# Output projections with tokens on the partitions: w_out and the FFN's down projection of a two-layer hybrid trunk

## The chip, the cores and the metric

The kernel runs on one core of one Trainium2 chip, as one program. The metric is the device time of a run, in microseconds (us). The kernel before takes 2708.34 us, the median of 3 runs (2707.84 to 2708.45).

## The reference

Two layers over 512 latent tokens with 256 context tokens ahead of them, width 1024. Each layer is a token-mixing sub-layer (an S5 state-space branch, windowed attention, a gated linear recurrence called HGRN2; merged by gates and put through `w_out`) and a convolutional FFN (2816 wide). Layer 0 gives 768 tokens (context and latent), layer 1 only the 512 latent ones. What matters here is what follows the two output projections: the norm of the result, its gain and gate, and the residual.

```python
def rmsnorm(x, g):
    return x * lax.rsqrt(jnp.mean(x * x, axis=-1, keepdims=True) + EPS) * g

def conv_ffn(h, w_up, conv_w, conv_b, w_down):
    u = depthwise_conv(h @ w_up, conv_w, conv_b)
    a, g = jnp.split(u, 2, axis=-1)
    return (jax.nn.silu(a) * g) @ w_down

for l in range(DEPTH):                      # latent tokens; the context rows go the same way in layer 0
    mod_l = jax.nn.silu(c) @ w_mod[l] + b_mod[l]
    sh1_l, sc1_l, g1_l, sh2_l, sc2_l, g2_l = jnp.split(mod_l, 6, axis=-1)
    hl = modulate(rmsnorm(xl, norm_g[l, 0]), sh1_l, sc1_l)
    ol, oc = mixing_sublayer(hl, hc, ...)   # ends with  @ w_out[l]
    xl = xl + g1_l * rmsnorm(ol, norm_g[l, 1])
    hl = modulate(rmsnorm(xl, norm_g[l, 2]), sh2_l, sc2_l)
    xl = xl + g2_l * rmsnorm(conv_ffn(hl, ...), norm_g[l, 3])
return xl
```

## The kernel before

Every fp32 product is made of three matmuls (hi by hi, lo by hi, hi by lo); `wload` brings a 128 by 1024 block of weights by DMA into a ring of three buffers `wr`, ScalarE writes its high part `wh`, VectorE the low part `wl` (three buffers each). All DMAs are issued by one queue on SyncE, in program order: one that waits holds up those behind it. Instructions are emitted by Python generators that `weave` interleaves at given paces, and a scheduler then sets each engine's order by priorities (`high_priority`, `lowly`); an engine works strictly in that order. All instructions are recorded by one helper line (L120; L118 in the changed kernel), so groups are told apart by tile names: `mm` and `mc` are PSUM for 512 and 256 columns, `pa` a two-bank PSUM tile, `pb` a PSUM bank with a single buffer, `slot` one of 52 SBUF buffers, `cst` the identity, `mscr` the scratch output of the modulation products, `rs_y`, `rs_v`, `rs_u`, `rs_h`, `xsv` small tiles of the reciprocal root, `cad`, `bbd`, `kd`, `tod`, `mt`, `mid` data of the S5 set-up.

The activations lie transposed, features on the partitions. In `w_out` and in the down projection the weights are stationary and the tokens stream: 512 latent columns into `mm` and, in layer 0, 256 context columns into `mc`. For `w_out` the first five blocks of output features go this way; the last three, and the last of the six groups of the down projection (`FG`, groups of 4, 4, 4, 4, 3, 3 blocks of 128 FFN features), go through `tail`: the weights are kept by `hold` in slots, and the tokens go in spans of 256 (two latent, then context), so that the residual of the first span can begin while the others are computed. The earlier groups of the down projection are summed in SBUF (`part`), one VectorE addition per block.

`out_evac` squares each block on ScalarE, scales it by the gain (modulation gate times norm weight, `amod`, one number per partition) on ScalarE and adds the squares up on VectorE (`oacc`). Features 0 to 511 are transposed back by TensorE as soon as they are there. `residual` then, for each pair of token tiles (a group), has TensorE sum the squares over the partitions by matmuls with `ones` into `pb`, transposes features 512 to 1023, and VectorE computes the reciprocal root (`mean_rstd`) and adds onto x. In three of the four cases the next norm follows (`x_scale`, `norm_part`): squares on ScalarE, a root, a scaling on VectorE, transposes, and then the next sub-layer's first products.

Two fillers run beside this. `mods_rows` computes modulation rows on VectorE; in layer 0's HGRN2 they are woven in at 1.6 per step, their weights coming through the `wr` ring. In layer 0's FFN `s5_setup(1)` gets 26 units of VectorE cost per up projection (`fs`), and then `s5_prep(1)` follows, 28 steps each of which loads blocks of `cad` and transposes them in a `pa` tile. The whole `prep` is drained by the end of the FFN.

## Time and profile before

| | us |
|---|---|
| median of 3 runs | 2708.34 |
| profiled execution: its time | 2715.15 |
| profiled execution: its span, first to last instruction | 2713.3 |
| TensorE busy | 2532.4 (93% of the span) |
| VectorE busy | 1898.0 (70%) |
| ScalarE busy | 1022.4 (38%) |
| mean granted TensorE clock | 0.976 of 2.4 GHz |

TensorE's busy time is that of overlapping, pipelined matmuls, so what a matmul costs is read from the start of one run of them to the start of the next, and what is missing from 100% is idle time, shown in brackets with its releaser. The stages follow each other in time: HGRN2 of layer 0 at about 340 to 700 us, its `w_out` at 880 to 960, its FFN at 1015 to 1600, the residual and norm that lead to layer 1 at 1600 to 1650, layer 1's FFN at 2350 to 2706.

### The profile page before, as it was taken

The page shows a single profiled execution, that of the slowest core. Times are in us where ns is not written, and L with a number is a line of the kernel's source. Part 1 is how long each engine was busy: PE and PEld are TensorE (multiplying, and loading weights), DVE is VectorE, ACT ScalarE, POOL GpSimd, SP SyncE. Part 2 cuts the span into 40 slices and gives each one's busy share as a digit, 9 for nine tenths or more (in the row PEclk, how much of TensorE's full clock was granted, in tenths as well). Part 3 has the DMA queues.
Part 4 walks back from the last instruction along what each step waited for, and adds up shares of the span by engine and source line. Part 5 has one row for each costly group of instructions (what it writes and reads, how often), then busy time and mean ns, then how long its engine had stood idle before and what let it go on. Part 6 is the DMA issues. An engine that isn't in the chain of part 4 may idle for free. (4 is left out here: it accounts for less than half of the span.)

```text
span 2713.3 us, 47072 instructions
## 1 busy us (share of the span) xinstructions
PE 2532.4 (93%) x18436; PEld 2128.1 (78%) x18436; DVE 1898.0 (70%) x4304; ACT 1022.4 (38%) x1813; POOL 121.1 (4%) x182
## 2 busy tenths in 40 slices
...
GB/s 245 128 129 112 140 143 161 148 177 134 180 197 213 111 133 142 163 117 125 119 142 144 118 136 215 147 82 92 105 117 131 168 214 163 146 95 97 98 95 99
DMA packets 239758, 381.36 MB, mean 141 GB/s; under 512 B 53648, under 2 KB 135984, under 8 KB 239536
## 3 DMA queue, kind: packets, MB, share of 16 engines
...
## 5 line engine op out<-in xcount | busy, mean ns | idle before, releaser
L120 PE MATMUL mm<-slot,wh 128*128 128x512 f32 (+1 forms) x3798 | 1200.7, 394 | 39.6 <-DVE slot L120 20.5
L120 PEld LDWEIGHTS mm<-slot,wh 128*128 128x128 f32 x3798 | 699.7, 190 | 177.2 <-DVE slot L120 24.9
L120 PE MATMUL mm<-slot,wl 128*128 128x512 f32 (+1 forms) x1899 | 742.7, 391 | 0.9 <-DVE wl L120 0.9
L120 DVE TENSOR_TENSOR slot<-slot,slot 128x384 f32<-128x384 f32 (+17 forms) x1340 | 665.8, 535 | 103.8 <-ACT slot L120 64.6
L120 PE MATMUL mc<-slot,wh 128*128 128x256 f32 (+1 forms) x3082 | 667.5, 310 | 12.8 <-ACT slot L120 10.2
L120 PEld LDWEIGHTS mc<-slot,wh 128*128 128x128 f32 x3082 | 519.0, 193 | 60.4 <-ACT slot L120 13.3
L120 DVE TENSOR_TENSOR wl<-wr,wh 128x1024 fp32r<-128x1024 f32 (+1 forms) x274 | 333.9, 1219 | 242.0 <-ACT wh L120 239.7
L120 ACT ACTIVATE wh<-wr 128x1024 fp32r<-128x1024 f32 (+1 forms) x274 | 288.5, 1053 | 525.9 <-PE mc L120 362.8
L120 PE MATMUL mc<-slot,wl 128*128 128x256 f32 (+1 forms) x1541 | 474.7, 308 | 0.0
L120 PEld LDWEIGHTS mm<-slot,wl 128*128 128x128 f32 x1899 | 360.6, 190 | 73.4 <-issue 2.6
L120 ACT ACTIVATE slot<-slot 128x768 fp32r<-128x768 f32 (+5 forms) x253 | 168.5, 669 | 383.3 <-DVE slot L120 329.7
L120 PEld LDWEIGHTS mc<-slot,wl 128*128 128x128 f32 x1541 | 297.4, 193 | 12.5
L120 PEld LDWEIGHTS pa<-slot,slot 128*32 128x32 f32 (+2 forms) x5696 | 212.5, 131 | 119.7 <-issue 60.5
L120 PE MATMUL pa<-slot,slot 128*32 128x32 f32 (+8 forms) x5696 | 254.6, 225 | 51.8 <-DVE slot L120 17.9
L120 ACT ACTIVATE slot<-mm 128x512 f32<-128x512 f32 (+1 forms) x180 | 103.6, 576 | 328.3 <-PE mm L120 288.2
L120 ACT ACTIVATE slot<-pa 128x512 f32<-128x512 f32 (+7 forms) x250 | 115.7, 493 | 238.3 <-PE pa L120 213.3
L120 PE MATMUL pa<-cst,slot 128*128 128x128 f32 x900 | 138.2, 282 | 30.6 <-DVE slot L120 20.4
L120 PEld LDWEIGHTS pa<-cst,slot 128*128 128x128 f32 x900 | 106.0, 144 | 58.3 <-issue 26.7
L120 PE MATMUL mm<-slot,slot 128*128 128x256 f32 (+1 forms) x784 | 110.7, 320 | 18.8 <-DVE xsv L120 16.2
L120 DVE SCALAR_TENSOR_TENSOR slot<-slot,slot 128x256 f32<-128x256 f32 (+7 forms) x129 | 92.4, 722 | 39.8 <-ACT slot L120 39.1
L120 DVE CUSTOM_DVE_ANT_0 mscr<-slot,slot 128x768 bf16<-128x768 f32 (+1 forms) x160 | 109.9, 687 | 14.3 <-DMA slot<-in_wmodt 12.0
L120 PEld LDWEIGHTS mm<-slot,slot 128*128 128x128 f32 (+1 forms) x784 | 92.9, 185 | 23.8 <-issue 18.2
...
## 6 DMA issues: line engine op xcount, KB each, us to landing
...
```

Source lines behind the costliest of these rows:

```text
L120: return _f(*(x.ap if isinstance(x, Slot) else x for x in a), **{k: x.ap if isinstance(x, Slot) else x for k, x in kw.items()})
```

## The change

Both output projections turn round: a block of 128 tokens of the activations is stationary, the weights stream, 512 output features at a time, and the result has tokens on the partitions. `out_proj` does `w_out` for each half of the features `f` and each pair of blocks `c`; `down` does one group for each half `f`, all token tiles, into `pa` tiles. A square with its row sum is then one ScalarE instruction (`accum_out`), and no transpose back and no sum over partitions is needed. The gain now varies along the columns: `out_state` transposes `amod` by two matmuls in `pb`, writes the rows to DRAM and loads them back onto all 128 partitions, and VectorE multiplies by them. `hold`, `tail`, `sums` and their buffers go. `FG` becomes 4, 4, 4, 4, 4, 2. Layer 0's modulation rows load into slots instead of the ring, are woven at 3 per step instead of 1.6 and drained by the end of the second head. `s5_prep(1)` uses `pb` and 4 blocks a step (36 steps), and `fs` is 22. Weights are laid out for this on the host.

```diff
-FG = [4, 4, 4, 4, 3, 3]
-DPER = {1: 8, 2: 4, 3: 2, 4: 2}
+FG = [4, 4, 4, 4, 4, 2]
...
-TL = (3, 3)
...
     def residual(self, l, which, oe, t0, nxt=None):
-            pso = self.pb()
-            self.sums(pso, oacc[0], g, True, False)
-            self.sums(pso, oacc[1], g, False, True)
-            y = self.mean_rstd(pso[:, g[0]:g[-1] + 1], len(g), "o")
-            pt = self.pa()
-            for j, t in enumerate(g):
-                for k in range(4):
-                    nc.tensor.transpose(pt[:, 512 * j + P * k:512 * j + P * k + P], o[4 + k][:, P * t:P * t + P], self.ident)
+            v = self.t(self.sm, [P, 8], "rsv")
+            nc.vector.tensor_add(v[:, :len(g)], ss[:, 0, g[0]:g[-1] + 1], ss[:, 1, g[0]:g[-1] + 1])
+            y = self.mean_rstd(v[:, :len(g)], len(g), "o")
+            o0 = {}
             for j, t in enumerate(g):
                 for f in range(2):
-                    src = pt[:, 512 * j:512 * j + 512] if f else o0[t]
-                    nc.vector.scalar_tensor_tensor(x[t][f], src, y[:, j:j + 1], x[t][f], ALU.mult, ALU.add)
+                    nc.vector.scalar_tensor_tensor(x[t][f], o[t, f], y[:, j:j + 1], x[t][f], ALU.mult, ALU.add)
                     dst = self.out[t - 2] if nxt is None else xd[t]
                     nc.sync.dma_start(dst[:, 512 * f:512 * f + 512], x[t][f])
+                o0[t] = o.pop((t, 0))
+                del o[t, 1]
...
+    def out_state(self, l, which, t0):
...
+        nv = 2 if t0 == 0 else 1
+
+        pt = self.pb()
+        a = self.s3(n=P)
+        gd = self.dr.tile([2, D], F32, name=self.nm("gain"))
+        for t in range(nv):
+            r = slice(32 * t, 32 * t + KT)
+            nc.tensor.matmul(pt[r, 0:P], self.amod[l][:, j, :, t], self.ident, start=True, stop=True)
+            nc.scalar.activation(a[r], pt[r, 0:P], AF.Copy)
+            nc.sync.dma_start(gd[t].rearrange("(k p) -> k p", p=P), a[r])
+        gain = {}
+        for t in range(nv):
+            for f in range(2):
+                gain[t, f] = self.s3(n=512)
+                nc.sync.dma_start(gain[t, f], gd[t, 512 * f:512 * f + 512].partition_broadcast(P))
+        return {"o": {}, "ss": self.t(self.sm, [P, 2, 8], "oss"), "gain": gain,
+                "groups": [range(s.start // P, s.stop // P) for s in self.spans(t0)]}
+
+    def out_evac(self, p, t, f, oe, part=None):
+
+        nc = self.nc
+        sq = self.s3(n=512)
+        o = oe["o"][t, f] = self.s3(n=512)
...
-            oe[0].pop(k, None)
+            for a, b, d in part:
+                nc.vector.tensor_add(o[:, a:b], d, p[:, a:b])
+            p = o
+        nc.scalar.activation(sq, p, AF.Square, accum_out=oe["ss"][:, f, t:t + 1])
+        nc.vector.tensor_mul(o, p, oe["gain"][0 if t >= 2 else 1, f])
+
+    def rows_product(self, out, x, w, j, t, first, last):
+
+        xh, xl = x
+        tk = slice(P * t, P * t + P)
+        wc = slice(512 * j, 512 * j + 512)
+        for i, (xt, wt) in enumerate(((xh, w[0]), (xl, w[0]), (xh, w[1]))):
+            self.nc.tensor.matmul(out, xt[:, tk], wt[:, wc], start=first and i == 0, stop=last and i == 2)
+
+    def out_proj(self, l, ms, oe):
+
+
+        groups = oe["groups"]
+        for f in range(2):
+            ps = {}
+            for g in groups:
+                if g[0] >= 2:
+                    pt = self.pa()
+                    for i, t in enumerate(g):
+                        ps[t] = pt[:, 512 * i:512 * i + 512]
+                else:
+                    for t in g:
+                        ps[t] = self.m1()
+            ws = []
+            for c in range(4):
+                ws.append(self.wload(self.I["wout"][l, f, c]))
+                if f == 0 or c == 0:
+                    for g in groups:
+                        for t in g:
+                            for j in range(2):
+                                self.rows_product(ps[t], ms[2 * c + j], ws[c], j, t, c + j == 0, 2 * c + j == KT - 1)
+                            if c == 3:
+                                self.out_evac(ps[t], t, f, oe)
+                    ws[c] = None
+            if f == 1:
+                for g in groups:
+                    for t in g:
+                        for c in range(1, 4):
+                            for j in range(2):
+                                self.rows_product(ps[t], ms[2 * c + j], ws[c], j, t, False, 2 * c + j == KT - 1)
+                        self.out_evac(ps[t], t, f, oe)
...
-        oe = {}, {}, []
-        for k in range(KT - TL[l]):
-            w = self.wload(I["wout"][l, k])
...
+        oe = self.out_state(l, 0, t0)
+        self.out_proj(l, ms, oe)
...
+        def down(gi, acts, oe=None):
             nonlocal chunk
             n = len(acts)
...
+            if gi == 0:
+                part.extend(self.s3() for _ in range(-(-4 * (NTILE - t0 // P) // 3)))
+            for f in range(2):
+                ws = [self.wload(I["wdn"][l, chunk + c]) for c in range(n // 2)]
+                chunk += n // 2
+                for g in groups:
+                    pt = self.pa()
+                    for x, t in enumerate(g):
+                        p = pt[:, 512 * x:512 * x + 512]
+                        for k in range(n):
+                            self.rows_product(p, acts[k], ws[k // 2], k % 2, t, k == 0, k == n - 1)
+                        if oe is not None:
+                            self.out_evac(p, t, f, oe, pieces(t, f))
+                            continue
+                        for a, b, d in pieces(t, f):
+                            if gi == 0:
+                                nc.scalar.activation(d, p[:, a:b], AF.Copy)
+                            else:
+                                nc.vector.tensor_add(d, d, p[:, a:b])
...
-            self.prep = self.lowly(self.s5_prep(1, self.pa, 8, self.sp), w["pb"])
+            self.prep = self.lowly(self.s5_prep(1, self.pb, 4, self.sp), w["pb"])
...
-        down(len(FG) - 1, prev)
+        oe = self.out_state(l, 1, t0)
+        down(len(FG) - 1, prev, oe)
+        part.clear()
...
-            mods = self.mods_rows(0, [i for i in range(4, 12) if i not in MLATE], 2, self.s3, True)
+            mods = self.mods_rows(0, [i for i in range(4, 12) if i not in MLATE], 2, self.s3)
...
-            self.weave(main, *g, (fill, w["hg"]), (prep, w["hp"]), (mods, 1.6))
+            self.weave(main, *g, (fill, w["hg"]), (prep, w["hp"]), (mods, 3))
+            if hh == 1:
+                self.drain(mods)
```

How it moves instructions, at the three places that matter. First TensorE at the end of layer 0's FFN. Before, the transposes of the first group's normed rows (`pa<-cst`) stand among the last products of the tail (`mm<-slot,slot`):

```order
L120 MATMUL mm_16697<-slot_2341_15953,slot_2414_16419 128x256
L120 MATMUL mm_16697<-slot_2358_16093,slot_2413_16418 128x256
L120 MATMUL mm_16697<-slot_2359_16094,slot_2413_16418 128x256
L120 MATMUL pa_16797<-cst,slot_2403_16377 128x128 [waits DVE_49,PE_49]
L120 MATMUL mm_16697<-slot_2358_16093,slot_2414_16419 128x256
L120 MATMUL pa_16797<-cst,slot_2404_16379 128x128 [waits DVE_49]
L120 MATMUL pa_16797<-cst,slot_2403_16377 128x128
```

After the change (names with L118), the last products of the down projection (`pa<-wh,slot`) come first, then four `pb` steps of `prep` with the transposes of the gain (`pb<-cst,amod`) in the second place, and only then the first group's transposes (the last row):

```order
L118 MATMUL pa_15939<-wh_15887,slot_2302_15507 128x512
L118 MATMUL pa_15939<-wl_15888,slot_2301_15506 128x512
L118 MATMUL pb_15593<-slot_2326_15594,slot_2323_15589 32x128 [waits DMAHW0_49,DMAHW1_49,Activation_49,Pool_49]
L118 MATMUL pb_15593<-slot_2326_15594,slot_2323_15589 32x128 x3
L118 MATMUL pb_15791<-cst,amod_114 8x128 [waits Activation_49] x2
L118 MATMUL pb_15963<-slot_2390_15964,slot_2323_15589 32x128 [waits DMAHW1_49,Activation_49]
L118 MATMUL pb_15963<-slot_2390_15964,slot_2323_15589 32x128 x3
L118 MATMUL pb_15978<-slot_2393_15979,slot_2323_15589 32x128 [waits DMAHW2_49,DVE_49]
L118 MATMUL pb_15978<-slot_2393_15979,slot_2323_15589 32x128 x3
L118 MATMUL pb_15986<-slot_2395_15987,slot_2323_15589 32x128 [waits DMAHW4_49,Activation_49]
L118 MATMUL pb_15986<-slot_2395_15987,slot_2323_15589 32x128 x3
L118 MATMUL pa_16084<-cst,slot_2358_15823 128x128 [waits DVE_49]
```

The gain's transposes, and a step of `prep` that shares their PSUM buffer and loads its data first, now stand behind the last product of the stage. On SyncE's queue the order there is: a weight load of the next layer, which waits for VectorE's `wl` in the list below (and that for a weight buffer which the last product frees), five transfers `tod` and `mt`, the loads of `bbd` and `cad` for the first `pb` step, and then the gain's two stores, two `cad` loads and the four loads of the gain rows.

On VectorE at the same place, before: additions onto the parts (`slot<-slot,mm`), the root's last steps and the first group's residual (`slot<-slot,rs_y,slot`, the later two of the group reading `pa`):

```order
L120 TENSOR_TENSOR slot_1911_12694<-slot_1911_12694,mm_16568 128x256 [waits PE_49]
L120 SCALAR_TENSOR_TENSOR rs_y_16739<-rs_u_16740,rs_y_16739 128x2 [waits DVE_49]
L120 TENSOR_TENSOR slot_2392_16313<-slot_2392_16313,slot_2434_16563 128x256 [waits Activation_49]
L120 SCALAR_TENSOR_TENSOR slot_2453_16710<-slot_2403_16377,rs_y_16739,slot_2453_16710 128x512 [waits DMAHW1_49,DVE_49]
L120 SCALAR_TENSOR_TENSOR slot_2455_16714<-slot_2404_16379,rs_y_16739,slot_2455_16714 128x512 [waits DMAHW3_49]
L120 TENSOR_TENSOR slot_1881_12473<-slot_1881_12473,mm_16581 128x256 [waits PE_49]
```

After: the last addition onto a part, a weight's low part, a row sum, a step of `prep` reading `pb`, and then the multiplications by the gain rows (the `slot` operand named second), whose first waits for a DMA:

```order
L118 TENSOR_TENSOR slot_2388_15959<-slot_1877_12173,pa_15939 128x512 [waits PE_49]
L118 TENSOR_TENSOR wl_16572<-wr_16570,wh_16571 128x1024 [waits DMAHW2_49,Activation_49]
L118 TENSOR_TENSOR rsv_16261<-oss_15808 128x2 [waits Activation_49]
L118 TENSOR_TENSOR slot_2324_15592<-slot_2324_15592,pb_15963 128x16 [waits DMAHW6_49,DMAHW1_49,DMAHW7_49,DMAHW0_49,Activation_49]
L118 SCALAR_TENSOR_TENSOR slot_2324_15592<-cst,pack,slot_2324_15592 128x16 [waits DVE_49]
L118 TENSOR_TENSOR slot_2358_15823<-slot_2358_15823,slot_2348_15800 128x512 [waits DMAHW3_49]
L118 TENSOR_TENSOR slot_2360_15835<-slot_2360_15835,slot_2348_15800 128x512
```

Ten more such multiplications follow before the first residual instruction `SCALAR_TENSOR_TENSOR slot_2397_16009<-slot_2358_15823,rs_y_16035,slot_2397_16009`; before, nothing of the kind stood there.

The third place is TensorE in layer 0's HGRN2, at the second head. Before, all steps of one head's recurrence (`pa`) follow each other with no product between them:

```order
L120 MATMUL pa_6515<-cst,slot_862_5624 128x128 [waits DVE_49,PE_49]
L120 MATMUL pa_6515<-cst,slot_862_5624 128x128 x4
L120 MATMUL pa_6523<-slot_792_5115,slot_952_6521 128x128 [waits Activation_49]
L120 MATMUL pa_6523<-slot_792_5115,slot_952_6521 128x128 x4
L120 MATMUL pa_6535<-cst,slot_891_5801 128x128 [waits DVE_49,PE_49]
L120 MATMUL pa_6535<-cst,slot_891_5801 128x128 x4
L120 MATMUL pa_6544<-slot_792_5115,slot_956_6541 128x128 [waits PE_49,Activation_49]
L120 MATMUL pa_6544<-slot_792_5115,slot_956_6541 128x128 x4
```

After, the same steps have products of the next head's input projection (`mm<-slot,wh`) between them:

```order
L118 MATMUL pa_6615<-cst,slot_898_5742 128x128 [waits DVE_49,PE_49]
L118 MATMUL pa_6615<-cst,slot_898_5742 128x128 x4
L118 MATMUL mm_6716<-slot_98_367,wh_6711 128x512
L118 MATMUL mm_6716<-slot_99_368,wh_6711 128x512
L118 MATMUL mm_6716<-slot_98_367,wl_6712 128x512
L118 MATMUL mm_6716<-slot_101_373,wh_6711 128x512
L118 MATMUL mm_6716<-slot_102_374,wh_6711 128x512
L118 MATMUL mm_6716<-slot_101_373,wl_6712 128x512
L118 MATMUL pa_6623<-slot_818_5200,slot_985_6621 128x128 [waits Activation_49]
L118 MATMUL pa_6623<-slot_818_5200,slot_985_6621 128x128 x4
L118 MATMUL pa_6635<-cst,slot_929_5928 128x128 [waits DVE_49,PE_49]
L118 MATMUL pa_6635<-cst,slot_929_5928 128x128 x4
```

## Rows read from the trace of the kernel before

**Rows 1.** The page: busy time of each engine, share of the span.

```profile
PE 2532.4 (93%) x18436; PEld 2128.1 (78%) x18436; DVE 1898.0 (70%) x4304; ACT 1022.4 (38%) x1813; POOL 121.1 (4%) x182
```

**Rows 2.** Windows: stretch, its length, busy us of each engine, PEclk, DMA share, GB/s.

```profile
core 0: us, PE busy (x) PEld busy (x) DVE busy (x) ACT busy (x) POOL busy (x), PEclk, DMA share, GB/s
340.00:700.00 360.00, 322.94 (x4238) 271.16 (x4239) 243.33 (x622) 85.08 (x191) 20.55 (x27) 0.96 0.50 153
597.00:650.00 53.00, 31.21 (x502) 27.00 (x502) 32.72 (x85) 7.67 (x23) 4.91 (x8) 0.81 0.47 154
620.00:625.00 5.00, 0.00 (x0) 0.00 (x0) 4.97 (x10) 0.62 (x2) 0.00 (x0) 0.50 0.00 0
1050.00:1350.00 300.00, 280.74 (x1593) 247.10 (x1592) 294.61 (x780) 117.71 (x174) 0.00 (x0) 0.97 0.45 135
1600.00:1650.00 50.00, 42.30 (x302) 38.97 (x301) 42.15 (x148) 29.80 (x73) 11.72 (x21) 0.93 0.54 172
2400.00:2650.00 250.00, 250.00 (x1104) 207.07 (x1104) 145.26 (x176) 91.71 (x114) 0.00 (x0) 1.00 0.30 96
```

**Rows 3.** Timeline of TensorE: start, us, instructions, count; products and transposes back to back.

```profile
1237.66 0.40 PE L120 MATMUL mc<-slot,wh 128*128 128x256 f32 x2
...
1238.01 0.40 PE L120 MATMUL mc<-slot,wh 128*128 128x256 f32 x2
...
2680.72 4.72 PE L120 MATMUL mm<-slot,slot 128*128 128x256 f32 x36
...
2696.06 1.36 PE L120 MATMUL pa<-cst,slot 128*128 128x128 f32 x11
```

**Rows 4.** Groups by form: busy us, mean ns, idle before.

```profile
L120 ACT ACTIVATE wh<-wr 128x1024 fp32r<-128x1024 f32 x266 | 281.7, 1059 | 520.2 <-PE mc L120 358.7 <-PE mm L120 105.6 <-issue 28.3
...
L120 DVE TENSOR_TENSOR wl<-wr,wh 128x1024 fp32r<-128x1024 f32 x266 | 326.3, 1227 | 238.7 <-ACT wh L120 237.4 <-DMA ud<-slot 0.4
...
L120 DVE TENSOR_TENSOR slot<-slot,slot 128x512 f32<-128x512 f32 x174 | 125.6, 734 | 23.7 <-ACT slot L120 14.3 <-POOL slot L120 4.5 <-DMA cad<-slot 3.0
...
L120 PE MATMUL pb<-ones,slot 128*128 128x1 f32 x80 | 11.8, 246 | 3.2 <-DVE slot L120 3.1
```

**Rows 5.** Timeline of TensorE in layer 0's HGRN2; in brackets idle time before and releaser.

```profile
612.65 1.51 PE L120 MATMUL pa<-cst,slot 128*128 128x128 f32 x6 [4.85 <-DVE slot L120]
...
625.03 0.79 PE L120 MATMUL mm<-slot,wh 128*128 128x512 f32 x1 [8.11 <-ACT slot L120]
```

**Rows 6.** Timeline of TensorE: layer 0's FFN, and layer 1's first residual.

```profile
1247.30 0.79 PE L120 MATMUL mc<-slot,wh 128*128 128x256 f32 x2 [3.86 <-ACT slot L120]
...
1266.95 1.22 PE L120 MATMUL mm<-slot,wh 128*128 128x512 f32 x2 [13.96 <-DVE slot L120]
...
2336.29 3.77 PE L120 MATMUL pa<-cst,slot 128*128 128x128 f32 x16 [8.46 <-DVE slot L120]
```

**Rows 7.** Timelines of SyncE, TensorE, VectorE: DMA issues, and a `prep` step from load to use.

```profile
605.39 1.95 SPq L120 DMA_DIRECT2D tod<-kd  x3
...
1385.00 0.59 SPq L120 DMA_DIRECT2D slot<-cad  x1
...
1388.27 0.64 PE L120 MATMUL pa<-slot,slot 128*32 128x128 f32 x16 [3.26 <-DMA slot<-cad]
...
1389.27 0.17 DVE L120 TENSOR_TENSOR slot<-slot,pa 128x16 f32<-128x16 f32 x1 [2.96 <-ACT slot L120]
```

**Rows 8.** Timelines of VectorE and TensorE at the residual between the layers, first group.

```profile
1608.24 1.41 DVE L120 SCALAR_TENSOR_TENSOR slot<-pa,rs_y,slot 128x512 f32<-128x512 f32 x2 [0.40 <-PE pa L120]
...
1613.89 1.67 DVE L120 TENSOR_SCALAR slot<-slot,rs_y 128x512 f32<-128x512 f32 x4
...
1614.84 1.84 PE L120 MATMUL pa<-cst,slot 128*128 128x128 f32 x15
1617.54 1.03 PE L120 MATMUL mm<-slot,wh 128*128 128x256 f32 x3 [0.86 <-POOL slot L120]
```

**Rows 9.** Timeline of VectorE: its last instruction, before the last stores.

```profile
2709.49 0.74 DVE L120 SCALAR_TENSOR_TENSOR slot<-pa,rs_y,slot 128x512 f32<-128x512 f32 x1
```

135 lines of the change are left out of this document (18 added, 117 removed).

## Prediction, made before the changed kernel was run

> **What bounds the kernel now.** I read the page's engine line first: TensorE is busy 2532.4 of 2713.3 us, VectorE 70% of the span [rows 1]. So the time is TensorE's work plus some 181 us in which it has none, and I went through the stretches looking for where that idle time lies and what ended it [rows 2]. In layer 1's FFN there is none: 250.00 of 250 us for 1104 matmuls. In layer 0's HGRN2 37 us of 360 are idle, and 22 of these in 597 to 650, where one head's steps wait for each other: 4.85 us for VectorE, then 8.11 us for ScalarE [rows 5], with VectorE on that chain 4.97 of 5 us in 620 to 625 [rows 2]. In layer 0's FFN VectorE is busy 294.6 of 300 us from 1050 to 1350 [rows 2]; it falls behind, and TensorE then waits 3.86 and 13.96 us [rows 6]. Between the layers 7.7 of 50 us are idle [rows 2]. So an edit is worth what it takes from TensorE's stream, except where a stall behind VectorE or a chain of small steps sets the pace.
>
> **Matmuls.** Columns streamed stay the same; 256-wide matmuls become 512-wide ones. A 512-wide one costs 250/1104 = 0.226 us [rows 2]. Three 256-wide ones take 1238.01 less 1237.66 = 0.35 us, 0.117 each, and in the tails 4.72/36 = 0.131 [rows 3]. By the code, layer 0's `w_out` has 120 at 512, 120 at 256 and 216 at 256 in the tail: 27.2 + 14.0 + 28.3 = 69.5 us; after, 288 at 512: 65.2. Layer 1: 120 and 144 in the tail, 46.0; after 192, 43.5. Down projection, layer 0: 456, 456 and 216 in the tail, 184.9; after 792, 179.3. Layer 1: 456 and 144, 122.1; after 528, 119.5. Saved: 4.3 + 2.5 + 5.6 + 2.6 = **15 us**.
>
> A rule speaks against that. The Trainium skill, "TensorE: Matmul & The Clock Gate", section "Back-to-back issue gap", gives 262 cycles for 256 columns and 518 for 512: 0.109 and 0.216 us at 2.4 GHz. By these figures the 1152 wide and 1296 narrow matmuls of before would take 390.1 us, the 1800 of after 388.5, and the change would save 1.6 us. The trace differs: its pairs of narrow ones cost 0.234 to 0.262 us and its wide ones 0.226, so the measurement decides for 15.
>
> **Transposes and sums.** The 160 transposes back (8 for each of 20 visits of a token tile) cost 1.36/11 = 0.124 us each [rows 3]: 19.8 us. Half of them stand in the residuals, where TensorE partly waits anyway; I count half of those: 15. The 80 sums by `ones` take 11.8 us [rows 4], of which I count 9, since the last ones of a stage lie in waits. Together **24 us**, between 15 and 31. On VectorE the additions of squares and on ScalarE the gain copies go, and 40 multiplications by a gain row at 0.734 us [rows 4] come; beside TensorE's stream they are hidden, except between the layers (below).
>
> **Layer 0's HGRN2.** The modulation rows are done two heads earlier, and the recurrence of the second head now has products of the next head's projection between its steps, as the order shows. The 13 us of waits there [rows 5] then lie beside work. I take **12 us**, between 0 (VectorE does the same modulation work in less time, and could be late itself) and 22 (the whole idle time of 597 to 650).
>
> **Layer 0's FFN.** The S5 set-up runs at 22 instead of 26 per up projection. VectorE's lag shrinks by about a seventh of its filler and the 18 us of waits [rows 6] shorten. I take **10 us**, between 0 and 18.
>
> **Between the layers: a loss.** After the change the gain rows are made behind the last product of layer 0's FFN, in a chain in which every step waits for the one ahead. TensorE has nothing else meanwhile. From the end of the last product:
> - the freed weight buffer is refilled, 1.06 us on ScalarE and 1.23 on VectorE [rows 4]: 2.3;
> - SyncE's load behind it and five transfers at up to 1.95/3 us [rows 7], say 0.5 each: 3.0;
> - the loads of `bbd` and `cad`: 0.6 to issue, and 3.3 from issue to use (1385.00 to 1388.27): 3.9;
> - the `prep` step, transposes to VectorE, 1388.27 to 1389.27 [rows 7], and the gain's own two transposes and copies at the same price: 2.0;
> - the store of the gain: the kernel's last store takes from 2709.49 + 0.74 to the end of the span at 2713.3 [rows 9], 3.1, plus the issue: 3.4;
> - the load of the rows, 3.3 as above with four issues: 3.7.
>
> That is 18.3 us. Then VectorE does 12 multiplications at 0.734 us [rows 4], all ahead of the first group's residual: 8.8. The group's four residual instructions take 2.8 (1.41 for two). From their end to the next layer's first product (1608.24 + 1.41 to 1617.54) it is 7.9 us, of which TensorE works some 1.9 [rows 8]: 6.0. Sum: 36 us idle. Before, the first group's waits at this place were about 2 us (0.86 of it shown in [rows 8]), because the tail's products covered the chain; the other 5.7 of the 7.7 I leave as they are. Loss 34, and about 1 us for the clock: after 5 us without work it is granted at 0.50, 1.2 GHz [rows 2], and 16 transposes after a wait of 8.46 take 3.77 us [rows 6] instead of 16 x 0.124 = 2.0. **Loss 35 us**, between 24 (transfers at half the price, residual and root partly beside the multiplications) and 45 (SyncE's queue held up once more).
>
> **Weight ring.** In a down group both weights of a half are needed for each token tile, and the ring has three buffers: the second weight of the second half reuses the first of the first half. By the order it is freed 8 matmuls before its successor is needed, 1.8 us, and the low part two matmuls later, 2.3; the conversion takes 1.06 + 1.23 = 2.3 us [rows 4] plus its hand-overs. Ten such places (five groups of four blocks, two layers) at about 0.5: **loss 5 us**. The bounds are 0, and 2.0 each (20) if the conversion stands behind other VectorE work, which it does in layer 0.
>
> **Preparation.** 36 steps through the one `pb` buffer instead of 28; such a step cost TensorE 3.26 us when its load was late [rows 7]. One or two more: **loss 4 us**, between 0 and 10. The other three residuals keep their cover but for a microsecond or so, which I count at nothing: their gain rows are made before the products end.
>
> **Sum.** -15 - 24 - 12 - 10 + 35 + 5 + 4 = -17 us against the profiled execution's 2715.15, so 2698; against the median of 2708.34, which lies 6.8 lower, **2691 us**.
>
> **Rivals.**
> (a) Both stalls go wholly, 22 and 18 us instead of 12 and 10: 18 more, 2673. For it: nothing in the order leaves a head's recurrence without products. Against: VectorE stays the busiest engine in the FFN's first half.
> (b) Slower: VectorE sets the pace. Its filler work is the same in sum, and if it is still behind in layer 0's FFN, the 22 us do not come and the ring's conversions queue behind the filler, 2 us at each of ten places instead of 0.5. Then -39 + 35 + 20 + 4 = +20: 2728; with the ring as forecast +5, 2713. The point at which it turns: with the ring at 20 us, the two stalls must give 20 of their 22 to break even. For it: 294.6 of 300 us busy [rows 2].
> (c) The narrow matmuls were no dearer in sum than the wide ones, so that only 1.6 us of the 15 come: 2704, no change to speak of. That is the rule cited above; the rows bear it out badly.
>
> **Chances.** Forecast (2678 to 2704) 0.42, (a) 0.15, (b) 0.30 (2713 to 2728), (c) 0.08, outside all of these 0.05. What a measurement of this kernel can tell from no change is about 0.2%, 5.4 us. Faster by more: 0.38 of the forecast, all of (a), 0.02 of (c), 0.03 of the rest, 0.58. Within: 0.04 of the forecast, 0.06 of (b), 0.06 of (c), 0.16. Slower: 0.24 of (b) and 0.02, 0.26. The range, 2668 to 2724, leaves out the far ends of (a) and (b) and the rest, less than 2 in 10; the likeliest case's own is 2678 to 2704.
>
> **What would show it.** In the profile after: between the layers a single idle time of TensorE of some 30 us, ended by VectorE, with multiplications ahead of the residual, and a DMA of the gain rows before them; in layer 0's HGRN2 no wait above 5 us; in the FFN one wait below 10 us where there were 18 in two; 528 matmuls of layer 1's down projection at 0.226 us. Wrong, if the idle time between the layers is under 20 or over 45 us, if VectorE still makes TensorE wait 18 us in the FFN, or if waits for `wl` appear at the halves of the down groups.

## Result, and the profile of the changed kernel

The changed kernel takes 2746.57 us (median, 2742.62 to 2748.39); the kernel before took 2708.09 us on the same chip. The ratio is 1.0126, 95% interval 1.0112 to 1.014: some 34 us slower, where 17 us faster was forecast. The page's engine line, which answers to [rows 1]:

```profile
PE 2519.8 (92%) x17560; PEld 2068.9 (75%) x17560; DVE 1897.1 (69%) x4290; ACT 981.5 (36%) x1732; POOL 121.2 (4%) x182
```

TensorE's work fell by 12.6 us (39 forecast), and its idle time rose from 180.9 to 226.8 us. The mean granted clock is 0.964, before 0.976. To see where, I cut both profiled executions (spans 2713.3 and 2746.6 us) at instructions that both have: the head norms of HGRN2, the last scan of S5, the start of the last run of outputs of each norm. Lengths in us, TensorE's idle time in brackets; the forecast is the terms of the sum put to their stages.

| stage | before | after | measured | forecast |
|---|---|---|---|---|
| start to the first head's norm | 408.3 (52.1) | 411.9 (49.5) | +3.6 | 0 |
| layer 0, HGRN2 | 279.6 (31.4) | 273.6 (27.9) | -6.0 | -12 |
| layer 0, rest of S5 | 110.2 (10.0) | 110.9 (11.2) | +0.7 | 0 |
| layer 0, merge, `w_out`, residual | 218.1 (4.3) | 220.3 (10.7) | +2.2 | -11.5 |
| layer 0, FFN and boundary to layer 1's norm | 630.7 (35.9) | 637.6 (50.0) | +6.9 | +18.7 |
| layer 1, S5 input and attention | 268.8 (11.4) | 290.2 (29.1) | +21.4 | 0 |
| layer 1, HGRN2 and S5 | 251.7 (10.4) | 251.6 (10.4) | -0.1 | 0 |
| layer 1, merge, `w_out`, residual | 171.0 (16.1) | 172.5 (21.6) | +1.5 | -7.3 |
| layer 1, FFN and the end | 374.9 (9.2) | 378.1 (16.4) | +3.2 | -4.9 |

**The boundary.** TensorE's timeline, after the last product of layer 0's FFN at 1592.56 us; it answers to [rows 8]:

```profile
1603.45 0.66 PE L118 MATMUL pb<-slot,slot 128*32 128x128 f32 x8 [10.89 <-DMA slot<-cad]
...
1609.76 0.66 PE L118 MATMUL pb<-slot,slot 128*32 128x128 f32 x8 [3.73 <-DMA slot<-cad]
...
1618.07 0.65 PE L118 MATMUL pb<-slot,slot 128*32 128x128 f32 x8 [6.42 <-DMA slot<-cad]
...
1626.92 0.47 PE L118 MATMUL pa<-cst,slot 128*128 128x128 f32 x1 [8.19 <-DVE slot L118]
```

29 us of idle time, where 36 were forecast. But three of the four waits are for `cad`: steps of layer 1's S5 preparation (`prep`) that are left over. By the order of the programs, its last matmuls stand behind the last product of the down projection. SyncE's timeline shows what its queue held there (start, us, kind, count), and how late the gain rows' store and load stand in it:

```profile
1594.75 0.33 SPq L118 DMA_DIRECT2D wr<-in_win  x1
1595.13 1.29 SPq L118 DMA_DIRECT2D tod<-kd  x2
...
1600.08 0.37 SPq L118 DMA_DIRECT2D slot<-cad  x1
...
1605.41 1.22 SPq L118 DMA_DIRECT2D gain<-slot  x2
1606.69 0.94 SPq L118 DMA_DIRECT2D slot<-cad  x2
1607.77 1.82 SPq L118 DMA_DIRECT2D slot<-gain  x4
```

**Layer 1's attention.** The largest loss lies a stage later, where no instruction was changed. Windows of the kernel after (stretch, length, busy us of each engine, clock, DMA share), the boundary, the attention's stage, and 30 us of it:

```profile
1592.60:1654.20 61.60, 29.29 (x193) 23.23 (x193) 40.20 (x125) 19.61 (x52) 8.77 (x16) 0.70 0.60 187
1654.20:1944.40 290.20, 261.15 (x1791) 204.30 (x1790) 164.97 (x357) 122.54 (x224) 20.11 (x22) 0.95 0.38 122
...
1717.00:1747.00 30.00, 16.80 (x73) 13.69 (x72) 26.94 (x40) 9.68 (x12) 8.30 (x5) 0.79 0.59 202
```

The same stage in the kernel before:

```profile
1646.90:1915.70 268.80, 257.38 (x1798) 201.64 (x1797) 160.64 (x353) 122.08 (x224) 19.53 (x23) 0.99 0.39 123
```

SyncE's timeline after shows why VectorE, idle for half of the 30 us before, is full in 1717 to 1747:

```profile
1650.53 0.80 SPq L118 DMA_DIRECT2D slot<-in_wmodt  x2
1651.39 1.97 SPq L118 DMA_DIRECT2D tod<-kd  x3
1663.70 5.81 SPq L118 DMA_DIRECT2D wr<-in_win  x3
```

Between 1653.4 and 1663.7 the queue stands before weight loads of layer 1, whose buffers VectorE has not given back; the modulation's weights (`in_wmodt`) are behind them. SyncE's waits (total, times, longest) in the 90 us around the boundary, first after, then before:

```profile
SPq L118 <- DVE wl L118: 25.3, 9, 10.3
...
SPq L118 <- DVE macc L118: 4.6, 3, 3.4
```

```profile
SPq L120 <- DVE macc L120: 29.3, 21, 4.3
SPq L120 <- DVE wl L120: 6.1, 6, 1.7
```

The queue did not wait less before, but it waited for the modulation's own sums (`macc`), at most 4.3 us at a time: its loads ran ahead of the products. After, they run behind. The last of the modulation's products on VectorE starts 31.5 us later than before (1771.7 against 1740.2), many of them come in a lump, and TensorE waits for what attention needs from VectorE and ScalarE:

```profile
1737.83 0.58 PE L118 MATMUL pa<-slot,slot 128*128 128x256 f32 x1 [6.95 <-DVE slot L118]
...
1745.51 0.79 PE L118 MATMUL mc<-slot,wh 128*128 128x512 f32 x1 [6.25 <-ACT slot L118]
...
1758.60 0.80 PE L118 MATMUL pa<-slot,slot 128*128 128x256 f32 x2 [5.47 <-ACT slot L118]
```

**The other stages.** TensorE's timeline in layer 0's HGRN2 (answers to [rows 5]), in layer 0's FFN (to [rows 6]) and in layer 1's `w_out` and its residual (to [rows 6]):

```profile
515.18 0.65 PE L118 MATMUL pb<-slot,slot 128*32 128x128 f32 x8 [8.92 <-DMA slot<-cad]
...
1252.71 0.79 PE L118 MATMUL pa<-wh,slot 128*128 128x512 f32 x1 [6.99 <-DVE slot L118]
...
2341.01 0.79 PE L118 MATMUL pa<-wh,slot 128*128 128x512 f32 x1 [4.30 <-DVE slot L118]
...
2366.34 0.87 PE L118 MATMUL pa<-cst,slot 128*128 128x128 f32 x2 [9.46 <-DVE slot L118]
```

The FFN's wait is 6.99 where there were 17.8 in two. In HGRN2 the waits of [rows 5] are gone, but one of 8.92 us for the preparation's transfers is new. In `w_out` 4.30 us are new. VectorE at the end (answers to [rows 9]), where the last product ends at 2733.8 us:

```profile
2736.45 2.74 DVE L118 SCALAR_TENSOR_TENSOR slot<-slot,rs_y,slot 128x512 f32<-128x512 f32 x4
...
2740.86 2.74 DVE L118 SCALAR_TENSOR_TENSOR slot<-slot,rs_y,slot 128x512 f32<-128x512 f32 x4
```

From TensorE's last instruction to the end it takes 12.8 us, before 7.1: both groups' residuals now lie behind the products.

### The profile page after: what moved, and what is told of

It reads as the page before. It is cut to its first block, busy times and chain, and to the rows that moved or that the text cites. A ratio compares the mean times of both kernels' runs of the same rounds, so it can differ in the third digit from the quotient of the medians.

```text
span 2746.6 us, 45237 instructions
## 1 busy us (share of the span) xinstructions
PE 2519.8 (92%) x17560; PEld 2068.9 (75%) x17560; DVE 1897.1 (69%) x4290; ACT 981.5 (36%) x1732; POOL 121.2 (4%) x182
## 5 line engine op out<-in xcount | busy, mean ns | idle before, releaser
L118 PE MATMUL mm<-slot,wh 128*128 128x512 f32 (+1 forms) x3160 | 998.4, 394 | 21.3 <-issue 7.0
L118 DVE TENSOR_TENSOR slot<-slot,slot 128x384 f32<-128x384 f32 (+16 forms) x1308 | 654.4, 540 | 77.9 <-ACT slot L118 39.6
L118 PEld LDWEIGHTS mm<-slot,wh 128*128 128x128 f32 x3160 | 582.6, 190 | 136.8 <-issue 11.1
L118 PE MATMUL mm<-slot,wl 128*128 128x512 f32 (+1 forms) x1580 | 618.1, 391 | 3.3 <-issue 2.4
L118 PE MATMUL mc<-slot,wh 128*128 128x256 f32 (+1 forms) x2568 | 556.1, 309 | 16.6 <-ACT slot L118 11.2
L118 DVE TENSOR_TENSOR wl<-wr,wh 128x1024 fp32r<-128x1024 f32 x284 | 348.3, 1227 | 313.0 <-ACT wh L118 310.2
L118 ACT ACTIVATE wh<-wr 128x1024 fp32r<-128x1024 f32 x284 | 301.0, 1060 | 610.7 <-PE mc L118 274.3
L118 PEld LDWEIGHTS mc<-slot,wh 128*128 128x128 f32 x2568 | 431.1, 193 | 55.0 <-ACT slot L118 13.2
L118 PE MATMUL mc<-slot,wl 128*128 128x256 f32 (+1 forms) x1284 | 394.1, 307 | 0.0
L118 PE MATMUL pa<-wh,slot 128*128 128x512 f32 x1136 | 359.4, 397 | 19.1 <-DVE slot L118 17.3
L118 PEld LDWEIGHTS mm<-slot,wl 128*128 128x128 f32 x1580 | 300.5, 190 | 63.2 <-issue 4.3
L118 PEld LDWEIGHTS pa<-slot,slot 128*32 128x32 f32 (+2 forms) x5568 | 214.1, 133 | 119.4 <-issue 58.9
L118 PE MATMUL pa<-slot,slot 128*32 128x32 f32 (+6 forms) x5568 | 252.7, 225 | 55.3 <-DVE slot L118 16.9
L118 ACT ACTIVATE slot<-slot 128x512 f32<-128x512 f32 (+4 forms) x233 | 164.5, 709 | 367.7 <-DVE slot L118 300.6
L118 PEld LDWEIGHTS pa<-wh,slot 128*128 128x128 f32 x1136 | 209.9, 189 | 77.2 <-DVE slot L118 26.9
L118 PEld LDWEIGHTS mc<-slot,wl 128*128 128x128 f32 x1284 | 247.1, 192 | 10.7 <-issue 0.4
L118 PE MATMUL pa<-wl,slot 128*128 128x512 f32 x568 | 223.3, 395 | 1.8 <-DVE wl L118 1.3
L118 DVE CUSTOM_DVE_ANT_0 mscr<-slot,slot 128x768 bf16<-128x768 f32 (+1 forms) x256 | 178.1, 696 | 35.3 <-DMA slot<-in_wmodt 29.5
L118 ACT ACTIVATE slot<-pa 128x512 f32<-128x512 f32 (+6 forms) x241 | 113.3, 499 | 239.2 <-PE pa L118 215.6
L118 ACT ACTIVATE slot<-mm 128x512 f32<-128x512 f32 x148 | 88.1, 595 | 274.2 <-PE mm L118 250.9
L118 PE MATMUL pa<-cst,slot 128*128 128x128 f32 x676 | 106.3, 289 | 32.4 <-DVE slot L118 22.0
L118 PEld LDWEIGHTS pa<-wl,slot 128*128 128x128 f32 x568 | 107.4, 189 | 27.4 <-DVE wl L118 4.9
```

What stands on the lines that cost most here:

```text
L118: return _f(*(x.ap if isinstance(x, Slot) else x for x in a), **{k: x.ap if isinstance(x, Slot) else x for k, x in kw.items()})
```

## Experiments

All ratios are to the kernel before on the same chip. A stage's length differs between executions by some microseconds even where its code is the same (HGRN2 of layer 0: 268.2 to 275.9 us in thirteen kernels), so one stage of one trace is read to about 4 us.

### The preparation that comes late

Theory: the set-up at 22 units per up projection instead of 26 ends later, the preparation after it is not through at the last product, and this makes both the boundary's loss and attention's. Rivals: the gain rows' chain, and the modulation's new pace. `fs26` gives the set-up its old pace:

```diff
-... "fs": 22 ...
+... "fs": 26 ...
```

> The changed kernel with one number set back: the S5 set-up in layer 0's FFN at 26 units per up projection instead of 22, so that the preparation for layer 1 begins three up projections earlier; in the order its last step and the gain's transposes then stand before the last product of the FFN. Theory A (the loss sits in the preparation and the gain rows that come after that product, and the slow start of layer 1's attention, 21 us longer than before, is their consequence): TensorE's idle time between the layers falls from 29 us to about 10, layer 1's stretch up to its HGRN2 falls from 290 to about 270 us, and some 8 us are lost again because VectorE falls behind earlier in the FFN: about 2712 us. Theory B (the slow start of layer 1 has another cause): only the idle time between the layers shrinks: about 2735 us.

2717.44 us, ratio 1.0023 (1.0009 to 1.0037): 28 of the 34 us are gone. The attention's stage takes 265.6 us, and of the four waits at the boundary one is left. The first wait of the FFN grew, however:

```profile
1258.70 0.80 PE L118 MATMUL pa<-wh,slot 128*128 128x512 f32 x1 [19.80 <-DVE slot L118]
...
1612.28 1.09 PE L118 MATMUL pa<-cst,slot 128*128 128x128 f32 x3 [8.48 <-DVE slot L118]
```

`late_prep_before` puts the late preparation alone into the kernel before:

```diff
-... "fs": 26 ...
+... "fs": 22 ...
...
-... self.s5_prep(1, self.pa, 8, self.sp) ...
+... self.s5_prep(1, self.pb, 4, self.sp) ...
```

> The kernel before with only the preparation changed as in the changed kernel: 22 units, 36 steps through the one pb buffer. No projection is turned and there is no gain row. Theory A: four preparation steps now stand behind the last product here too; the first group's chain waits for them and the transfers behind them, and layer 1's start becomes some 20 us longer: 2708 + 20 + 10 less 8 in the FFN, about 2730 us. Theory B: layer 1's start stays as before, and the smaller backlog of VectorE shows: about 2702 us.

2725.71 us, ratio 1.0056 (1.0034 to 1.0078). Its attention stage and SyncE's waits in the 90 us around the boundary:

```profile
1640.60:1932.70 292.10, 266.09 (x1797) 207.89 (x1796) 164.03 (x356) 122.55 (x224) 20.44 (x22) 0.94 0.38 120
```

```profile
SPq L120 <- DVE wl L120: 27.0, 9, 10.3
```

The whole loss of attention, with no projection turned. At the boundary TensorE waits for the late steps there too:

```profile
1599.34 0.65 PE L120 MATMUL pb<-slot,slot 128*32 128x128 f32 x8 [6.94 <-DMA slot<-cad]
...
1610.88 1.44 PE L120 MATMUL pb<-ones,slot 128*128 128x1 f32 x6 [4.02 <-DVE rs_v L120]
```

The FFN's stage is shorter than before all the same (625.1 against 630.7 us), since the waits of [rows 6] at its first products, 17.8 us, fell to 4.28. That the wait at the boundary is longer in the changed kernel, where the order leaves TensorE nothing else to do, is likely the turned order's part; no run separates the two.

`gain_early` makes the gain rows before the last group's up projections, at the pace of 22:

```diff
+            if gi == len(FG) - 1:
+                oe = self.out_state(l, 1, t0)
             for j in range(n):
...
-        oe = self.out_state(l, 1, t0)
         down(len(FG) - 1, prev, oe)
```

> The changed kernel with one line moved: the gain rows of layer 0's FFN are asked for before the last two up projections; the last four preparation steps stay behind the last product. Theory A: the store and load of the gain and the 12 multiplications leave the chain between the layers, the late preparation stays with its queue of transfers: idle time there 29 to about 15 us, layer 1's start still some 20 us too long: about 2732 us. If the gain rows alone made the loss, both go: about 2708. Theory B: as A for the first part, 2732 us, so this run tells the gain from the preparation, not A from B.

2740.42 us, ratio 1.0108 (1.0085 to 1.0131), 5 us by the ratios, whose intervals overlap, and nothing of attention (292.8 us). The boundary's waits were to fall to 15 us and still add up to 29:

```profile
1598.19 0.65 PE L118 MATMUL pb<-slot,slot 128*32 128x128 f32 x8 [10.72 <-DMA slot<-cad]
1604.64 0.65 PE L118 MATMUL pb<-slot,slot 128*32 128x128 f32 x8 [5.79 <-DMA slot<-cad]
...
1620.31 1.94 PE L118 MATMUL pa<-cst,slot 128*128 128x128 f32 x7 [12.68 <-DVE slot L118]
```

With the preparation late, the gain rows are not what is waited for. `mods_old` undoes the modulation's change in layer 0:

```diff
-    mods = self.mods_rows(0, ..., 2, self.s3)
+    mods = self.mods_rows(0, ..., 2, self.s3, True)
...
-    self.weave(..., (mods, 3))
-    if hh == 1:
-        self.drain(mods)
+    self.weave(..., (mods, 1.6))
```

> The changed kernel with the modulation rows of layer 0 as before (weights through the ring, 1.6 per step, no early end). Theory A: the idle time between the layers and layer 1's start stay as in the changed kernel, HGRN2 of layer 0 gets its 22 us of waits at 597 to 650 back and loses the new wait of 8.9 us at 515: 2746 to 2760 us. Theory B with the modulation change as the other cause (slots held or transfers moved): layer 1's start falls back to 270 us: about 2730 us.

2749.09 us, ratio 1.0142 (1.0118 to 1.0166). So that is no cause. `fs24` takes 24 units, with the preparation ending some 90 matmuls before the last product:

> The changed kernel with fs 24 in place of 22: layer 1's preparation ends some 90 matmuls before the last product of layer 0's FFN, where fs 26 ends it 270 before. Theory: only that the preparation is through before the last product counts, and a faster set-up costs by the VectorE work that it piles up in front of the FFN's first groups (one wait of 7.0 us with fs 22, of 19.8 us with fs 26). Then this kernel keeps the end of the boundary and the short attention of layer 1 (about 266 us, not 290) and its VectorE wait falls to 10 to 16 us: 2705 to 2715 us, 3 to 8 below fs 26. Rival: the preparation's last transfers must be off SP's queue well before the boundary; then layer 1's attention is long again (280 to 290 us) and the time 2725 to 2740 us.

2720.55 us, ratio 1.0031 (1.0018 to 1.0045), no better than 26. Attention stays short (265.9 us), so the preparation needs only to be through by the last product. But the time forecast was missed: the first wait fell to 11.28, and the boundary's rose to 24.50:

```profile
1251.13 1.22 PE L118 MATMUL pa<-wh,slot 128*128 128x512 f32 x2 [11.28 <-DVE slot L118]
...
1617.67 3.86 PE L118 MATMUL pa<-cst,slot 128*128 128x128 f32 x16 [24.50 <-DVE slot L118]
```

### Two terms of the sum, each alone

`narrow` is `fs26` with each turned product of 512 columns as two of 256:

```diff
-            self.nc.tensor.matmul(out, xt[:, tk], wt[:, wc], ...)
+            for q in range(0, 512, 256):
+                self.nc.tensor.matmul(out[:, q:q + 256], xt[:, tk], wt[:, 512 * j + q:512 * j + q + 256], ...)
```

> The changed kernel with fs 26, and each of the turned projections' products of 512 columns as two of 256, so that 1704 matmuls become 3408. The prediction's term: a matmul of 256 columns takes 0.131 us and one of 512 takes 0.227 us, so that two narrow ones cost 0.03 us more: 45 to 60 us longer than fs 26, by the clear stages some 9 us in layer 1's w_out and 15 to 18 us in its FFN. Rival (c of the prediction, to which the 4 us of gain point): narrow matmuls are no dearer by the column, 0 to 8 us longer in all, and layer 1's FFN within 3 us of 378 us.

2734.9 us, ratio 1.0091 (1.0072 to 1.0109), by the ratios 18 us over `fs26`; layer 1's FFN 382.7 against 378.0 us. Both expectations missed; the answer lies between. The engine lines, first `fs26`, then `narrow`:

```profile
PE 2508.0 (93%) x17560; PEld 2057.9 (76%) x17560; DVE 1893.8 (70%) x4290; ACT 979.7 (36%) x1732; POOL 121.5 (4%) x182
```

```profile
PE 2532.8 (93%) x19360; PEld 2168.1 (79%) x19360; DVE 1893.5 (69%) x4290; ACT 980.4 (36%) x1732; POOL 122.4 (4%) x182
```

1800 more matmuls (the expectation's 1704 leave out 96 of the context's) and 24.8 us more: a pair costs 0.014 us more than the one it replaces, and with 0.226 for that one [rows 2] a narrow matmul costs 0.120, not the 0.131 that I took for the tails.

`before_mods_new` puts the modulation's change alone into the kernel before (the removed and added lines of `mods_old` the other way round).

> The kernel before with layer 0's modulation into slots, at the pace of 3 and drained with the second head pair, as in the changed kernel, and no projection turned. The prediction's term: 12 us less in layer 0's HGRN2 (279.6 us before), 2696 us. Rival, from the run with the old modulation in the changed kernel: the waits on the modulation's ring go, but the preparation's transfers (cad) then come late for TensorE in the same place, and the stage falls by 2 to 4 us only: 2703 to 2708 us.

2708.87 us, ratio 0.9985 (0.9971 to 1.0), about 4 us at an interval that reaches 1: the rival. HGRN2 takes 275.6 us there, in the four kernels with the old modulation and the old projections 277.1 to 279.6.

### The cover

About 24 us of TensorE's work are gone in `fs26` (2532.4 to 2508.0), and the time did not fall. Theory: they came back as idle time, since the loop over the halves `f` is outside the loop over tokens: every token group ends in the last half pass, and the first group's residual has 12 matmuls of cover in the FFN. `tokens_last` (on `fs26`) turns the loops of the last down group:

```diff
+            if oe is not None:
+                wf = [[self.wload(I["wdn"][l, chunk + f * (n // 2) + c]) for c in range(n // 2)] for f in range(2)]
+                for g in groups:
+                    pts = [self.pa(), self.pa()]
+                    for x, t in enumerate(g):
+                        for f in range(2):
...
+                            self.out_evac(p, t, f, oe, pieces(t, f))
+                return
```

> The changed kernel with fs 26, and in the last down group of both layers the loop over tokens outside the loop over halves, so that the first token group is done with both halves before the second begins. Theory (cover): the products' gain came back as idle time because every token group ends in the last half pass, so that the residual of the first has 12 matmuls of cover; with 24 matmuls between the groups' ends, the wait of 8.5 us before layer 1's norm shrinks by 3 to 6 us, and the end behind the last product, 13.2 us, by 2 to 4 us: 6 to 10 us under fs 26. Rival: VectorE paces the last groups (two additions, a multiplication and four residual instructions of 0.7 us for each token tile), and the order of the products changes nothing: within 3 us of fs 26.

2715.96 us, ratio 1.0013 (0.9999 to 1.0027): by the ratios 3 us better than `fs26`, with intervals that overlap: the rival rather than the theory. The boundary's one wait of 8.48 became two:

```profile
1601.24 0.73 PE L118 MATMUL pa<-wh,slot 128*128 128x512 f32 x2 [2.43 <-DVE slot L118]
1608.91 3.86 PE L118 MATMUL pa<-cst,slot 128*128 128x128 f32 x16 [4.63 <-DVE slot L118]
```

`hp0` (on `fs24`) and `before_hp0` (on the kernel before) take away the raised rank of the first two groups' residual:

```diff
-HP = (150, 100)
+HP = (0, 0)
```

> The changed kernel with fs 24, and without the raised rank of the residual's first two groups, so that VectorE takes the additions and gain multiplications of the later group, and its root, ahead of or between the four residual instructions of the group before. Theory (cover): the last products wait for a PSUM buffer that VectorE gives back behind the first group's residual; with the order turned the waits of 4.3 us in layer 1's w_out and some 2 us of the end go, 3 to 8 us under fs 24. Rival: the residual's chain of the first group is what TensorE waits for next (the transposes of the norm), and delaying it costs what the earlier buffers give: within 3 us of fs 24 or slower.

2711.67 us, ratio 1.0001 (0.9987 to 1.0015), 8 us better than `fs24` in the same comparison. In layer 1 the wait of 4.30 us is now 1.65 (its stage 169.3 us, `fs24` 174.6); in layer 0 the `w_out` stage gains 9.8 us, of which the FFN's stage gives 5.2 back (to the last output of each norm, whose last run is shorter in this order).

```profile
2302.69 0.73 PE L118 MATMUL pa<-wh,slot 128*128 128x512 f32 x2 [1.65 <-DVE slot L118]
```

> The kernel before without the raised rank of the residual's first two groups, and nothing else. Theory (cover): there the last group's products were long enough to cover the first group's residual, so the rank is worth something or nothing: 0 to 5 us slower than before. Rival: the rank was a loss in the kernel before too, and its removal is no mending of the turned order: 3 to 8 us faster.

2728.15 us, ratio 1.006 (1.0038 to 1.0082): 16 us slower, more than expected, and the other sign than in the turned kernel. Layer 0's `w_out` stage takes 226.8 us (218.1 before). A rank that was right for the old order is wrong for the turned one. `tl_hp0` has all three mendings, `fs` 26, `tokens_last` and `hp0`:

> The changed kernel with fs 26, tokens outermost in the last down group, and the residual's raised rank taken away: the three mendings together. Theory (cover): the three gains lie in different places (boundary, the last FFN's end, the two w_outs) and add: 3 us from the tokens' order, 5 to 9 us from the rank, 2700 to 2708 us, 0.2 to 0.4 per cent under the kernel before. Rival: the two act on the same wait, the last group's residual on VectorE, and the second adds nothing: 2708 to 2715 us, not to be told from before.

2709.17 us, ratio 0.9992 (0.998 to 1.0003): the rival, they do not add. Layer 0's `w_out` gains 8.9 us on `fs26`, the FFN behind it loses 9.6.

### VectorE in layer 0's FFN

Whatever I mended, TensorE's idle time in that stage stayed at 40 to 52 us. In `fs26` VectorE is 98% busy up to 1320 us, then half idle. `tl_hp0_low` gives the set-up work on it a lower rank:

```diff
-    ..., self.s5_setup(1)), w["ah"]), 300)
+    ..., self.s5_setup(1)), w["ah"]), 900)
```

> The same three mendings, and the set-up work of layer 0's FFN at a lower rank (900 in place of 300) on VectorE. Theory: the wait of 19 us before the first down products comes from set-up instructions that stand ahead of the FFN's own additions on a VectorE that is 98 per cent busy; with the FFN's first, that wait falls by 5 to 15 us, and so does the time. Rival: the work is only put off to the preparation, whose end moves some 100 matmuls towards the boundary: the wait appears there, as with fs 24, within 4 us of the kernel with the three mendings.

2698.79 us, ratio 0.9953 (0.9934 to 0.9971), 10 us better than `tl_hp0`. The first wait is gone, and both sides were right in part, since one at the boundary is there:

```profile
1604.86 3.86 PE L118 MATMUL pa<-cst,slot 128*128 128x128 f32 x16 [26.85 <-DVE slot L118]
```

> The three mendings and the set-up at rank 1800. Theory: the rank of 900 has taken out what there is of the first wait, and the order of the set-up hardly changes beyond it: within 4 us of 2699 us. Rival: more of the wait goes, 3 to 8 us below.

2699.21 us, ratio 0.9952 (0.9937 to 0.9966): nothing more in it. `before_low` has the rank alone in the kernel before:

> The kernel before with the set-up work of layer 0's FFN at rank 900 in place of 300, and no projection turned. Theory: its wait of 13.96 us on VectorE at 1266.95 us is the same backlog of set-up work as the 19.8 us of the mended kernel, and falls by 5 to 14 us: 2695 to 2705 us; the gain of the three mendings with this rank over before is then no merit of the turned projections. Rival: in the kernel before the set-up's rank is right as it is (the preparation, in smaller steps on the other PSUM buffers, comes late instead): within 5 us of before, or slower.

2701.78 us, ratio 0.9954 (0.9938 to 0.997). The rank gives the kernel before as much as the mended one leads by: its wait at 1266.95 [rows 6] is gone and the other is smaller.

```profile
1249.29 0.50 PE L120 MATMUL mc<-slot,wh 128*128 128x256 f32 x2 [1.93 <-DVE slot L120]
...
1606.98 1.84 PE L120 MATMUL pb<-ones,slot 128*128 128x1 f32 x8 [12.07 <-DVE rs_u L120]
```

`before_low_mods` adds the modulation of `before_mods_new`:

> The kernel before with the set-up of layer 0's FFN at rank 900 and with the changed kernel's modulation in layer 0 (slots, pace 3, drained with the second head pair); no projection turned. Theory: the two gains, 12 us in the FFN and 4 us in HGRN2, lie in different stages and add: 2694 to 2700 us, 0.5 to 0.65 per cent under before. Rival: the earlier modulation only moves the preparation's transfers, and the gain is the rank's alone: 2700 to 2704 us.

2699.59 us, ratio 0.9943 (0.9927 to 0.9959), with `tl_hp0_low` the fastest; the interval doesn't tell it from the rank alone. `fs26_low` has the rank on `fs26`:

> The changed kernel with fs 26 and the set-up at rank 900, without the tokens' order and with the residual's raised rank. Theory: the set-up's rank is worth 8 to 13 us by itself, as it was with the other mendings (2709 to 2699 us): 2704 to 2710 us. Rival: it only pays where the tokens' order covers the boundary, since the preparation ends 96 matmuls nearer to it; then 2715 to 2722 us, with the boundary's wait at 15 to 25 us, as with fs 24.

2712.51 us, ratio 0.9996 (0.9983 to 1.001): between the two, with the boundary's wait of the rival. TensorE waits 24.60 us, and VectorE, 9.95 of them, for the gain rows, the chain that I had forecast:

```profile
1619.10 1.30 PE L118 MATMUL pa<-cst,slot 128*128 128x128 f32 x4 [24.60 <-DVE slot L118]
```

```profile
1606.68 0.69 DVE L118 TENSOR_TENSOR slot<-slot,slot 128x512 f32<-128x512 f32 x1 [9.95 <-DMA slot<-gain]
```

`low_gain` and `best` add the edit of `gain_early` to `fs26_low` and to `tl_hp0_low`.

> The changed kernel with fs 26, the set-up at rank 900 and the gain rows made before the last group's up projections; tokens innermost and the residual's rank raised as in the changed kernel. Theory (the forecast's chain): the wait of 24.60 us at the boundary, with 9.95 us of VectorE's for the load of the gain rows in it, falls to 8 to 13 us: 2698 to 2704 us, below the kernel before. Rival: as above, 2709 to 2713 us.

> The kernel with the three mendings and the set-up at rank 900, and the gain rows made before the last group's up projections. Theory (the forecast's chain): in the kernel without this TensorE waits 26.85 us at the boundary, of which VectorE stands some 10 us for the load of the gain rows, and the transposes of the gain stand 82 matmuls before the last product; made a group earlier, the wait falls to 9 to 15 us and the time to 2684 to 2692 us, 0.75 to 1.0 per cent under the kernel before. Rival: what ends that wait is the preparation or the residual's own arithmetic (12 multiplications and the roots on VectorE), as in the run of the changed kernel with the gain early, which gained 4 us: 2694 to 2699 us.

`low_gain` 2714.53 us, ratio 1.0015 (1.0002 to 1.0028), not to be told from `fs26_low`; `best`, against its name, 2704.91 us, ratio 0.9978 (0.9969 to 0.9987), some 7 us slower than `tl_hp0_low`. In both the wait at the boundary did shrink. In `tl_hp0_low` VectorE waits for the gain rows and then multiplies by them, all ahead of the first residual:

```profile
1588.20 7.32 DVE L118 TENSOR_TENSOR slot<-slot,slot 128x512 f32<-128x512 f32 x12 [7.34 <-DMA slot<-gain]
```

With the rows made early no such wait is left, and TensorE's falls from 24.60 to 19.05 us in `low_gain` and from 26.85 to 14.44 in `best`. So the gain rows do hold part of the boundary there. But in `best` their chain costs elsewhere: ScalarE waits for the gain's store, which SyncE's queue issues at 1569.51 us, some 25 us after the gain's transposes, and TensorE waits behind ScalarE. First ScalarE, then TensorE:

```profile
1572.57 0.60 ACT L118 ACTIVATE slot<-mm 128x512 f32<-128x512 f32 x1 [7.08 <-DMA gain<-slot]
```

```profile
1573.49 0.79 PE L118 MATMUL mc<-slot,wh 128*128 128x256 f32 x2 [5.84 <-ACT slot L118]
1583.49 1.79 PE L118 MATMUL pa<-wh,slot 128*128 128x512 f32 x3 [5.13 <-ACT slot L118]
```

The stage in windows, `tl_hp0_low` and then `best`:

```profile
1001.29:1629.60 628.31, 586.03 (x3224) 492.77 (x3223) 506.11 (x1224) 254.23 (x413) 17.42 (x33) 0.98 0.46 140
```

```profile
1006.41:1641.54 635.13, 592.19 (x3224) 496.20 (x3223) 506.12 (x1224) 254.04 (x412) 17.34 (x33) 0.97 0.45 139
```

The idle time is the same (42.3 and 42.9 us), but the same matmuls take 6.2 us more, about what `best` lost by the ratios. It is the granted clock, whose lower level is 0.50, 1.2 GHz. In `tl_hp0_low` it was 0.50 in 1590 to 1600 us, when TensorE had no work. In `best` it was 0.66 in 1570 to 1590 us, behind the new waits and with TensorE busy 11.4 of the 20, and 0.57 in 1620 to 1630 us with 7.0 of 10 busy, where `tl_hp0_low` has 1.00.

What is left of the wait in `best` is VectorE's: its timeline has less than 1 us of idle time in any gap from 1585.74 to the residual at 1606.88, where the parts' additions, the 12 multiplications and the roots follow each other. That this arithmetic sets the pace of the rest is what the two runs speak for; no run took it away, so it is not shown.

## Why the prediction was wrong

**The step that failed: "Preparation".** "One or two more: loss 4 us" counted the steps that the preparation has more and not where they end. With the set-up slower, it was not through at the last product. `fs26` and `late_prep_before` show what that cost: 21 us in layer 1's attention, which had no term, and the waits for `cad` at the boundary. With the old pace the boundary's waits fall from 29 to 8.48 us, of which the FFN's first wait takes 13 back. I had read the slower set-up as a gain (the FFN's wait, right at 10 and measured at 10.8), and did not ask what queued behind it: the preparation, behind that SyncE's queue, behind that layer 1's modulation. That the last two links carry the loss is read from the timelines; the runs vary the preparation alone.

**Between the layers**: forecast 36 us of idle time, measured 29, so the size is about right, and the cause only in part: three of the waits were the preparation's. With it mended the wait is 8.5 us; where the preparation then ends nearer to the boundary (`fs24`, `hp0`, `fs26_low`, `tl_hp0_low`, `tl_hp0_low2`), 24 to 27, with VectorE waiting 5.8 to 9.95 us for the load of the gain rows in each: there the forecast's chain is seen. The whole stage came out 12 us better than its terms.

**Matmuls: 15 forecast, 4 measured** (the products' times from start to start, before against `fs26`). 1296 narrow ones at the 0.120 of `narrow` and 1800 wide ones at 0.226 give 155.5 - 648 x 0.2264 = 8.8, so 6 of the 11 us of the miss are the price of the narrow matmuls, taken from a row with other gaps in it: in the same trace the median from one `mm<-slot,slot` of 256 columns to the next is 0.120. Of the other 5, wider gaps in the new blocks are a part, about 2.8 us for twelve in layer 1's FFN where 2.72 were due. The estimate by the Trainium skill ("TensorE: Matmul & The Clock Gate", section "Back-to-back issue gap") in the prediction, 1.6, was nearer than mine from the row.

**Transposes and sums**: 24 forecast, 20 measured (11 and 9).

**HGRN2**: 12 forecast, 6 measured in this pair, 2 to 5 by `mods_old` and `before_mods_new`. What is missing lies ahead of the stage: from the start to the first head's norm the fifteen kernels with the new modulation take 409.1 to 414.0 us, the five with the old one 407.0 to 408.3. Nothing was forecast there, and why it is longer is not shown. The waits named went as forecast; the transfers of `cad` came late at the same heads. This was one of the bounds' mechanisms (0 us, "could be late itself"), not the value.

**Weight ring**: 5 forecast; TensorE's waits for `wl` at the turned products add up to 1.8 us, 1.35 of them one wait in layer 0.

**"The other three residuals keep their cover but for a microsecond or so, which I count at nothing"** failed too. The two `w_out` stages and layer 1's FFN, forecast at -23.7 us, came out at +6.9: idle time of 6.4, 5.5 and 7.2 us more (5.7 of the last behind the last product), and less work saved. Of the 50 us between forecast and measurement this is the larger part, 31, and attention's 21 the other; `fs26` mends the second of the two alone. Nobody had to wait for the gain rows in these stages; that the residuals lost the products beside them fits `hp0`, which gave 8 us back, but `tokens_last` gave 3 at most, so this cause is in part argued.

**The rivals.** (b) had the sign and named VectorE, but not this way: the ring's conversions cost 2, not 20. What made the kernel slower, a transfer queue held up beyond the boundary, was among none of them. The range ended 23 us below the time.

**What is left of the change.** `tl_hp0_low` against `before_low`: TensorE busy 2502.2 against 2534.9 us, 32.7 less; idle 192.3 against 165.8, 26.5 more; the ratios 0.9953 and 0.9954 are the same. Of the idle time 15 us more lie in layer 0's FFN, 7 in layer 1's and its end, 5 and 3 in the two `w_out` stages. Turning the projections took the work off TensorE and left the time to VectorE and to the order. Where in layer 0's FFN this idle time could be avoided stays open.
